# Seven products of quarters for eight in a decoder layer's output projection

## The chip, the cores and the metric

One core of one Trainium2 chip runs the kernel. The metric is the device time in microseconds, as the median of several executions. A core has a matrix engine (TensorE, PE in the profile), three engines for elementwise work (VectorE or DVE, ScalarE or ACT, GpSimd or POOL) and SyncE (SP), which issues most transfers. Each engine works through a queue of its own in order and waits on semaphores for the others. Matrix products accumulate in banks of PSUM, 128 rows of 512 floats each, which VectorE and ScalarE read.

## The reference

One decoder layer on 512 rows of width 1024, in float32. Cut to what matters here:

```python
u = rmsnorm(x, ln1_g)
q, k, v, pool_in, z, xbc, dt_raw, gate_pre = split(u @ w_in)
y_a = attention(q, k, v) @ w_a; y_b = pooling(pool_in) @ w_b; y_c = ssd(z, xbc, dt_raw) @ w_c
gates = sigmoid(gate_pre + b_gate)                       # three of width 1024
merged = gates[0] * y_a + gates[1] * y_b + gates[2] * y_c  # 512 x 1024
x = x + merged @ w_o                                     # the product changed here, w_o 1024 x 1024
x = x + conv_ffn(rmsnorm(x, ln2_g), ...)                 # up, depthwise conv, silu gate, down
out = rmsnorm(x, final_g)
```

## The kernel before, in words

The layer's rows are kept as four row blocks of 128, the columns as two halves of 512. A float32 product is made of three: each operand is split into a rounded high part and a remainder, and high x high, high x low and low x high are accumulated in one bank (`mm3`, L223 on; all its matmuls have line 236). Weights come through a pipeline of jobs (`Job`, the loop at the end of the function): while job n runs its matmuls, VectorE makes the remainder `wl` of job n+1 (`low`, L215), ScalarE casts the high part `wh` of job n+2 in two cuts (`cast`, L195), and SyncE fetches the raw weights of job n+3 (`fetch`, L182). There are two buffers for raw weights, three for `wh` and two for `wl`, so a step of this pipeline also waits for the buffer's former reader. Four engines (TensorE, ScalarE, VectorE, GpSimd) take their instructions in the order in which the program writes them out; SyncE's are placed by the framework. A list `running` holds generators, pieces of elementwise work that are carried on by one piece at each `step()`; the job bodies call `step()` after a bank or two. `after(n, it)` delays a piece by n steps.

Other products of the kernel already use 7 products of quarters where 8 would do (`Seven`, and `down_group` in the FFN). Rows of one operand and weights are then cut in quarters, and sums of quarters are multiplied; `sums_of` (L322 on) makes the four sums of an operand that are needed: four additions of half rows on VectorE, two casts on ScalarE, two remainders on VectorE.

The stage around the change:

- `branch_jobs(2, w_c, ...)`: four jobs of 48 matmuls, each two column blocks m of the branch's result. For each m, VectorE multiplies by the gate (L1226) and adds to the merged branches `MG[m]` (L1227), ScalarE casts the high part `mgh` (L1230), VectorE makes the remainder `mgl` (L1231).
- `load_x1`: SyncE loads both rows of norm gains and the eight pieces of x, `X1[tb, h]`.
- `wo_jobs(pair, h)`: the output product, for two row blocks (`pair`) and one half of the columns (`h`) at a time, in two jobs of four k each; 8 jobs of 24 matmuls. Each job fetches its 1 MB of w_o, so w_o is loaded twice. A finished bank is added to x by VectorE (L1252). After the first half, `norm_early` squares it on ScalarE and multiplies by the gain on GpSimd (L462). After the second half, `norm_late` squares that one (L437), takes the square root on ScalarE (L471, with a table load), forms the factor in four small VectorE operations (L486 to L490) and scales both halves into `us`. `norm_turn` then transposes them on TensorE (L451, 8 transposes a row block), and ScalarE and VectorE take high part and remainder out (L454, L455). For the first pair this comes a step later; for the second it is put into the opening of the FFN.
- `up_jobs`: the FFN. Its first two jobs (`opening`, L1421) begin with the columns of the first two row blocks while the norm of the last two is finished.

Of the kernel before, what the change touches and what calls it, by code (L numbers as in the profile page):

```python
# [10 lines left out]
F32 = mybir.dt.float32  # L11
F32R = mybir.dt.float32r
# [4 lines left out]
P = 128  # L17
S = 512
# [64 lines left out]
def trunk(ctx: ExitStack, tc, out, x, rel_bias, ln1_g, w_in, b_gate, w_a, pool_w, pool_scale, w_b,  # L83
# [370 lines left out]
            act.copy(hh, pv)  # L454
            dve.tensor_sub(ul[:, 4 * h:4 * h + 4, tb * P:(tb + 1) * P], pv, hh.bitcast(F32))  # L455

    def norm_early(t, g):

        ss, v0, xg = small("ss", [P, 1]), cpool.tile([P, 1], F32, name=f"v0_{len(V0)}"), T("xg")
        squares(act, t, ss)  # L460
        dve.tensor_scalar(v0, ss, 1.0 / D, EPS, OP.mult, OP.add)
        pool.tensor_tensor(xg, t, g[0], OP.mult)  # L462
        V0.append(v0)
        return v0, xg

    def norm_late(t, g, v0, outs, last=None):


        ss, v, sq, r, rt = (small(n, [P, 1]) for n in ("ss", "v", "sq", "r", "rt"))
        squares(act, t, ss)  # L470
        act.activation(sq, ss, AF.Sqrt, bias=v0, scale=1.0 / D)  # L471
        xg = T("xg")
        dve.tensor_tensor(xg, t, g[1], OP.mult)
        if last:
            dve.scalar_tensor_tensor(v, ss, -0.5 / D, last, OP.mult, OP.add)
            yield xg

            dve.reciprocal(r, sq)
            dve.scalar_tensor_tensor(rt, r, v, r, OP.mult, OP.mult)
            dve.scalar_tensor_tensor(rt, rt, 1.5, r, OP.add, OP.mult)  # L480

            (o1, x1), (o0, x0) = outs(xg)
            act.mul(o0, x0, rt)
            dve.tensor_scalar(o1, x1, rt, None, OP.mult)
            return
        dve.scalar_tensor_tensor(v, ss, 1.0 / D, v0, OP.mult, OP.add)  # L486
        yield xg
        dve.reciprocal(r, sq)
        dve.scalar_tensor_tensor(rt, r, v, r, OP.mult, OP.mult)
        dve.tensor_scalar(rt, rt, -0.5, 1.5, OP.mult, OP.add)  # L490
        for o, src in outs(xg):
            dve.tensor_scalar(o, src, r, rt, OP.mult, OP.mult)

    V0 = []

# [708 lines left out]
                    dve.tensor_sub(YT[q][1], Y[gi][:, q % 4, :], YT[q][0].bitcast(F32))  # L1204


    MG, MH, SG = {}, {}, {}

    def gate_jobs(b, lo=0, hi=8):
        def evac(m, ps):  # L1210
# [5 lines left out]

        return jobs_a(w_in, C_GATE + b * D + lo * P, hi - lo, uhk, ulk, KD, evac)

    def branch_jobs(b, w, parts, nk, last=False, more=()):
        def evac(m, ps):  # L1220
            if b == 1:
                MG[m] = T("yo")
                act.copy(MG[m], ps)
                return
            s = SG[b, m]
            dve.tensor_tensor(s, s, ps, OP.mult)  # L1226
            (dve if last else pool).tensor_tensor(MG[m], MG[m], s, OP.add)  # L1227
            if last:
                h, l = T("mgh", F32R), T("mgl", F32R)
                act.copy(h, MG[m])  # L1230
                dve.tensor_sub(l, MG[m], h.bitcast(F32))  # L1231
                MH[m] = (h, l)
# [8 lines left out]

    def load_x1():
        nxt["g2"] = grow(ln2_g[0])
        for tb in range(4):
            for h in range(2):
                t = X1[tb, h] = T("x1")
                sp.dma_start(t, x[tb * P:(tb + 1) * P, h * S:(h + 1) * S])

    def wo_jobs(pair, h):
        def evac(tb, ps):  # L1250
            t = X1[tb, h]
            dve.tensor_tensor(t, t, ps, OP.add)  # L1252
            if h == 0:
                nxt[tb] = norm_early(t, nxt["g2"])
                return
# [3 lines left out]
            v0, xg0 = nxt[tb]  # L1259
            us = [T("u0"), T("u1")]  # L1260
            it = norm_late(t, nxt["g2"], v0, lambda xg1: ((us[0], xg0), (us[1], xg1)))
# [20 lines left out]
        return jobs_b(lambda k0, k1: [wsrc(w_o, k0, k1, h * S, h * S + S)], S,  # L1282
                      lambda k, tb: MH[k][0][:, tb * P:(tb + 1) * P],
                      lambda k, tb: MH[k][1][:, tb * P:(tb + 1) * P], KD, evac,
                      blocks=(2 * pair, 2 * pair + 1), turn_over=pair == 1 and h == 1)


    ACTS = {}
    ff = {}
# [177 lines left out]
    def down_jobs(h):  # L1467

        def evac(tb, ps):
            t = X1[tb, h]  # L1470
            dve.tensor_tensor(t, t, ps, OP.add)
            if h == 0:
                running.append(early(tb))
                return
            v0, vh, xg0 = fin[tb]
            for _ in norm_late(t, fin["g"], v0, lambda xg1: ((xg1, xg1), (xg0, xg0)), last=vh):
# [14 lines left out]
    def program():  # L1491
# [21 lines left out]
        for group, next_ in zip(groups, groups[1:] + (None,)):  # L1513
# [4 lines left out]
            for i, job in enumerate(group.jobs):  # L1518
# [13 lines left out]
        yield from gate_jobs(0)  # L1532
        many = {"a": branch_jobs(0, w_a, AO, 3), "g": gate_jobs(2),
                "Z": z_jobs(0), "z": z_jobs(1)}
        for token in MIX:
            if token in many:
                yield next(many[token])
            else:
                yield Call(lambda i=int(token): waiting.append(y_norm(i)))
        yield Call(finish)  # L1540
        yield from branch_jobs(2, w_c, YT, 8, last=True)
        yield Call(load_x1)
        for pair in range(2):
            for h in range(2):
# [239 lines left out]
```

## Time and profile before

| what | value |
|---|---|
| median of 3 executions | 1021.73 us (1021.33 to 1021.78) |
| the profiled execution | 1021.86 us |
| its span in the trace | 1019.9 us |
| granted TensorE clock, mean | 0.998 |
| instructions | 13619 |

The page gives busy time by engine, the span in 40 slices, the chain of work that ended last, and the costliest groups of instructions by line. The timeline lists one engine's instructions in order: start, time, engine, line, operation, output and inputs, shapes, and in brackets the idle time ahead of it with what ended it. A name such as `pb` is the program's name of a tile: `pa` the banks of the w_c product, `pb` those of the output product, `pu` those of the FFN, `uT` transposes. Matmuls are pipelined, so a row's time is longer than the distance to the next row; the distances are used here.

### The profile page before, as it was taken

The numbers are of one execution on the slowest core, as the hardware profiler recorded it, in microseconds if no ns is written. First come the engines' busy times: TensorE is split into PE (matmuls) and PEld (weight loads), VectorE is DVE, ScalarE is ACT, GpSimd is POOL, SyncE is SP. The second block draws the span as 40 slices with busy tenths as digits, with TensorE's granted clock in tenths as the row PEclk, the third lists the DMA queues.
The fourth block names the chain that finished last, engine by engine and source line by source line (L and its number), as shares of the span: only waits on it lengthen the run. The fifth ranks groups of instructions, "written<-read, shape, count | busy, mean of one in ns | idle before, by whom it ended". The sixth has DMA issues, their size and how long they took to land.

```text
span 1019.9 us, 13619 instructions
## 1 busy us (share of the span) xinstructions
PE 1010.3 (99%) x5402; PEld 862.2 (85%) x5402; DVE 707.4 (69%) x886; ACT 511.3 (50%) x863; POOL 136.4 (13%) x120
## 2 busy tenths in 40 slices
PE   8999999999999999999999999999999999999997
PEld 8998878999988888888888888898888888888885
DVE  6564768577767647666889665768778768685756
ACT  5433546564435476879467224554444444433434
POOL 1691000010000000000052501102111100111002
PEclk9999999999999999999999999999999999999999
DMA  8548222255254344552253427532332322321332
GB/s 270 170 101 210 92 74 76 58 149 162 91 183 113 91 124 104 145 141 87 81 155 127 165 85 272 163 124 83 105 102 83 106 101 83 123 83 42 124 103 82
DMA packets 115629, 123.34 MB, mean 121 GB/s; under 512 B 6483, under 2 KB 96150, under 8 KB 115567
## 3 DMA queue, kind: packets, MB, share of 16 engines
q1 hardware_dynamic: 113247, 119.01, 37.5%
q0 software_dynamic: 1728, 2.62, 1.5%
q8 instruction: 42, 0.69, 0.3%
q10 hardware_dynamic: 592, 0.86, 0.2%
q14 instruction: 20, 0.16, 0.0%
HBM read 118.68 MB, written 3.00 MB: 119 GB/s over the span
## 4 chain that ended last, share of the span: by engine, by line
PE 98%; DMA 1%; DVE 0%; ACT 0%; ACTq 0%; issue 0%
PE pa L236 36%; PE pu L236 22%; PE pb L236 12%; PE pd L236 7%; PE pqk L236 6%; PE pq L236 3%; PE pa L1632 2%; PE ps L786 1%; PE pu L1421 1%; PE ppw L236 1%; PE po L834 1%; PE pt L820 1%; PE py L1119 1%; DMA xin<-in_x_dram 1%; PE pyo L1126 1%; PE pst L1107 0%
## 5 line engine op out<-in xcount | busy, mean ns | idle before, releaser
L215 DVE TENSOR_TENSOR wl<-raw,wh 128x2048 fp32r<-128x2048 f32 (+3 forms) x92 | 214.1, 2328 | 51.5 <-ACT wh L195 38.8
L195 ACT CAST wh<-raw 128x1024 fp32r<-128x1024 f32 (+4 forms) x181 | 181.4, 1021 | 57.4 <-DVE raw L359 17.8
L1316 DVE SCALAR_TENSOR_TENSOR hc<-pu,fcol,hc 128x510 f32<-128x510 f32 x88 | 65.9, 748 | 56.2 <-ACT hc L1313 54.5
L236 PE MATMUL pa<-uh,wh 128*128 128x512 f32 (+1 forms) x368 | 88.8, 381 | 0.0
L236 PE MATMUL pa<-ul,wh 128*128 128x512 f32 (+1 forms) x368 | 86.8, 375 | 0.0
L236 PE MATMUL pa<-uh,wl 128*128 128x512 f32 (+1 forms) x368 | 86.8, 375 | 0.0
L236 PE MATMUL pu<-uh,wh 128*128 128x512 f32 (+1 forms) x352 | 83.5, 379 | 0.0
L236 PE MATMUL pu<-ul,wh 128*128 128x512 f32 (+1 forms) x352 | 83.5, 379 | 0.0
L236 PE MATMUL pu<-uh,wl 128*128 128x512 f32 (+1 forms) x352 | 83.5, 379 | 0.0
L236 PEld LDWEIGHTS pa<-ul,wh 128*128 128x128 f32 x368 | 66.7, 188 | 12.6
L236 PEld LDWEIGHTS pa<-uh,wl 128*128 128x128 f32 x368 | 66.7, 188 | 12.5
L236 PEld LDWEIGHTS pa<-uh,wh 128*128 128x128 f32 x368 | 65.4, 189 | 11.8
L236 PEld LDWEIGHTS pu<-ul,wh 128*128 128x128 f32 x352 | 64.2, 188 | 12.5
L236 PEld LDWEIGHTS pu<-uh,wl 128*128 128x128 f32 x352 | 64.2, 188 | 12.5
L236 PEld LDWEIGHTS pu<-uh,wh 128*128 128x128 f32 x352 | 64.1, 188 | 12.4
L1313 ACT ACTIVATE hc<-pu,fcol,fcol 128x512 f32<-128x512 f32 x40 | 31.2, 779 | 78.9 <-PE pu L236 78.9
L1321 POOL TENSOR_TENSOR hc<-hc 128x512 f32<-128x512 f32 x22 | 30.8, 1400 | 289.1 <-DVE hc L1316 244.4
L808 ACT ACTIVATE sb<-sb,nmls 128x128 f32<-128x128 f32 (+1 forms) x72 | 30.0, 418 | 31.4 <-DVE nmls L805 20.8
L215 DVE TENSOR_TENSOR wl<-w,wh 128x2048 fp32r<-128x2048 f32 (+1 forms) x18 | 38.0, 2111 | 10.2 <-issue 4.6
L1102 POOL TENSOR_TENSOR st<-st,dts 128x512 f32<-128x512 f32 x4 | 4.2, 1052 | 225.6 <-ACT st L1110 163.5
L195 ACT CAST wh<-w 128x1024 fp32r<-128x1024 f32 (+1 forms) x36 | 32.9, 954 | 2.4 <-DVE w L341 2.4
L1318 ACT ACTIVATE hc<-hc 128x512 f32<-128x512 f32 x22 | 13.9, 633 | 40.2 <-DVE hc L1316 40.2
(409 smaller groups left out, 1924.4 us busy)
## 6 DMA issues: line engine op xcount, KB each, us to landing
raw<-in_w_in_dram SPq DMA_DIRECT2D x24, 1024.0 KB, 5.8
raw<-in_ffn_w_up_dram SPq DMA_DIRECT2D x22, 1024.0 KB, 5.7
raw<-in_w_o_dram SPq DMA_DIRECT2D x8, 1024.0 KB, 5.1
raw<-in_ffn_w_down_dram SPq DMA_DIRECT2D x8, 1024.0 KB, 5.3
raw<-in_w_in_dram SPq DMA_DIRECT2D x14, 512.0 KB, 5.5
raw<-in_w_in_dram SPq DMA_DIRECT2D x8, 768.0 KB
raw<-in_w_b_dram SPq DMA_DIRECT2D x4, 1024.0 KB
w<-in_ffn_w_down_dram SPq DMA_DIRECT2D x4, 1024.0 KB, 5.0
```

What stands on the lines that cost most here:

```text
L195: (other.tensor_copy if other and i else act.copy)(job.high[:, :, o], job.raw[:, :, o])
L215: (eng or dve).tensor_tensor(l[:, :, o], job.raw[:, :, o], h[:, :, o].bitcast(F32), OP.subtract)
L236: pe.matmul(ps, l, r, start=first and n == 0, stop=last and n == total - 1, skip_group_check=onto)
L786: pe.matmul(pss[i][:, o:o + w * P], q[r, n * P:(n + 1) * P], k[r, kb * P:(kb + w) * P], start=True, stop=True)
L808: act.activation(sb[:, off:off + w * P], sb[:, off:off + w * P], AF.Exp, bias=nm[:, n, h:h + 1], accum_out=ls[:, n, h:h + 1])
L820: pe.transpose(pt[:, o:o + P], sb[:, o:o + P], eye)
L834: pe.matmul(po[DH * hh:DH * hh + DH, n * P:(n + 1) * P], V[g, kb + i][:, (2 * c + hh) * DH:(2 * c + hh + 1) * DH], probs[2 * c + hh, nb][: ...
L1313: act.activation(t, ps, AF.Identity, bias=ff["c1"][:, ff["b"] + m:ff["b"] + m + 1], scale=fw(2, m))
L1316: dve.scalar_tensor_tensor(t[:, sh:], ps[:, :S - sh], fw(k, m), t[:, sh:], OP.mult, OP.add)
L1318: act.activation(t, t, AF.Silu)
L1321: pool.tensor_tensor(a, a, t, OP.mult)
L1632: pe.matmul(first[2 * n + j][:, lo:hi], a[:, k, j * P:(j + 1) * P], b[:, k, lo:hi], start=a is wh and b is uh and k == 0, stop=a is wl and ...
```

## The change

The 8 jobs of `wo_jobs` are replaced by the 7 of `wo_group`. Merged branches and w_o are cut in quarters: the rows of w_o in even and odd blocks of 128 (`two`), its columns in halves; the merged branches in the same blocks and in two halves of the rows. Every product is 2 row blocks x 4 k x 3 = 24 matmuls of 512 columns, on a pair of banks. They run in the order two, five, three, one, six, seven, four. `three` goes on in the banks of `five`; `six`, `seven` and `four` go on in those of `one`, and after each of them the banks are read while they still accumulate. Row blocks 0 and 1 are complete after `six`, 2 and 3 after `four`.

Of x, four pieces are loaded as before and added to by VectorE. The other four (`fresh`) are copied out of the bank by ScalarE, and x is added by an accumulating transfer that GpSimd issues. The norm's first half is now the one that is complete first, so `norm_early` and `norm_late` take its number; in the new form (`apart`) the late half is scaled by factor and gain in one VectorE operation, the early one by ScalarE.

Sums of weights: one by accumulating transfers (`plus`, four pieces of 256 KB), three by VectorE: `W[2]` in the w_c stage (`sums`), `W[1]` behind the remainder of `one`, and the sum of `four` when its cast is made, that is, while `six` is prepared. Sums of the merged branches are made in the w_c stage and at the start of the product (`merged`); `two` and `five` (`apart`) take their last k after the first three of both banks. One weight load for this product, `W[0]`, stands ahead in SyncE's queue where one of the FFN's stood, and so do three buffers of that pool, which the FFN's sums now get after it.

```diff
-    def norm_early(t, g):
+    def norm_early(t, g, h=0):
...
-    def norm_late(t, g, v0, outs, last=None):
+    def norm_late(t, g, v0, outs, last, h=1, apart=False):
...
+        xg = None
+        if not apart:
+            xg = T("xg")
+            dve.tensor_tensor(xg, t, g[h], OP.mult)
+        dve.scalar_tensor_tensor(v, ss, -0.5 / D, last, OP.mult, OP.add)
         yield xg
+
         dve.reciprocal(r, sq)
         dve.scalar_tensor_tensor(rt, r, v, r, OP.mult, OP.mult)
+        dve.scalar_tensor_tensor(rt, rt, 1.5, r, OP.add, OP.mult)
+
+        if apart:
+            o1, (o0, x0) = outs()
+            dve.scalar_tensor_tensor(o1, t, rt, g[h], OP.mult, OP.mult)
+            act.mul(o0, x0, rt)
+            return
...
+    def merged(m):
+        if m % 2 == 0:
+            t = T("m0", F32R)
+            act.copy(t[:, :256], MG[m][:, LO])
+            dve.tensor_sub(t[:, 256:], MG[m][:, LO], t[:, :256].bitcast(F32))
+            MH[m] = (t[:, :256], t[:, 256:])
+            return
+        h, l = T("mgh", F32R), T("mgl", F32R)
+        act.copy(h, MG[m])
+        it = sums_of(MG[m - 1], MG[m], T("sah", F32R), T("sal", F32R),
+                     lambda j, h, l: MS.__setitem__((j, m // 2), (h, l)), True)
+        if m < 7:
+            next(it)
+        dve.tensor_sub(l, MG[m], h.bitcast(F32))
+        MH[m] = (h, l)
+        if m > 6:
+            next(it)
+        yield
+        yield from it
...
+        for tb, h in ((0, 1), (1, 1), (2, 0), (3, 0)):
+            t = X1[tb, h] = T("x1")
+            sp.dma_start(t, x[tb * P:(tb + 1) * P, h * S:(h + 1) * S])
+
+    def wo_group():
...
+        def load():
+            for two in (0, 1):
+                W.append(ypool.tile([P, 4, S], F32, name="w3", tag="xs"))
+                sp.dma_start(W[-1], quarter(two, 1))
+            plus(0, 0, 0)
+
+        def plus(i, two, h):
+            for k in range(4):
+                pool.dma_start(W[i][:, k, :], quarter(two, h)[:, k, :], accum_op=OP.add)
+
+        def sums():
+            W.append(ypool.tile([P, 4, S], F32, name="w3", tag="xs"))
+            dve.tensor_tensor(W[2], W[0], W[1], OP.add)
+
+        def first(tb, h):
+            half = 1 - h
+            v0, xg = norm_early(X1[tb, half], nxt["g2"], half)
+            vh = cpool.tile([P, 1], F32, name=f"vo{tb}")
+            dve.tensor_scalar(vh, v0, -0.5, None, OP.mult)
+            nxt[tb] = v0, vh, xg
+
+        def then(tb, h):
...
-            if pair == 0:
+            if tb < 2:
                 r = rest()
                 next(r)
                 running.append(after(1, r))
...
+        def job(j, raw, form, bank, outs, more=False, op=OP.add, behind=None, apart=False, fresh=False):
...
+                def read(i):
+                    tb = 2 * hi + i
+                    if fresh:
+                        t = X1[tb, h] = T("x1")
+                        act.copy(t, bank[i])
+                        pool.dma_start(t, x[tb * P:(tb + 1) * P, h * S:(h + 1) * S],
+                                       accum_op=OP.add)
+                        return
+                    t = X1[tb, h]
+                    dve.tensor_tensor(t, t, bank[i], op)
+                    if behind:
+                        behind(tb, h)
+
+                if apart:
+                    for i in range(2):
+                        product(i, range(3), True, False)
+                    step()
+                    parts = side(j)
+                    for i in range(2):
+                        product(i, (3,), False, True)
+                        read(i)
+                    step()
+                    return
+                for i in range(2):
+                    product(i, range(4), True, True)
+                    read(i)
+                    step()
...
+        two = job("A12", quarter(1, 0), None, B, (0, 0), apart=True, fresh=True)
+        five = job(1, None, lambda: W[0], B, (1, 1), apart=True, fresh=True)
+        three = job(4, None, lambda: W[1], B, (0, 1), more=True)
+        one = job("A11", quarter(0, 0), None, A, (0, 0), behind=lambda tb, h: first(tb, 1))
+        six = job(2, None, lambda: W[2], A, (0, 1), more=True, op=OP.subtract, behind=then)
+        seven = job(3, None, lambda: W[1], A, (1, 1), more=True, op=OP.subtract,
+                    behind=lambda tb, h: first(tb, 0))
+        four = job("A22", quarter(1, 0), lambda: total(four.raw, four.raw, W[2]), A, (1, 0), more=True,
+                   behind=then)
+        one.then = lambda: total(W[1], W[2], one.raw, OP.subtract)
+        four.late, inner = True, four.body
...
-        yield from branch_jobs(2, w_c, YT, 8, last=True)
-        yield Call(load_x1)
-        for pair in range(2):
-            for h in range(2):
-                yield from wo_jobs(pair, h)
-            if pair == 0:
+        for i, job in enumerate(branch_jobs(2, w_c, YT, 8, last=True)):
+            if i == 1:
+                yield Call(sums)
+            if i == 3:
+                yield Call(load_x1)
+            yield job
+        for i, job in enumerate(group):
+            yield job
+            if i == 3:
                 yield Call(ff_cols)
...
-MIX = "ZZ0zz1ggggaa"
+MIX = "ZZ0zz1ggggwaa"
```

`four` is marked late: it is prepared as the old last job was (`late_split`), and its own preparation, the remainder of the FFN's first weights among it, is split over its end and the opening.

More of the change, by code (lines that the diff above doesn't have):

```diff
@@ L1228, in evac @@
             if last:
[L1229 to L1232, printed above, removed]
+                running.append(merged(m))
         return jobs_a(w, 0, 8, lambda k: parts[k][0], lambda k: parts[k][1], nk, evac,
@@ L1280, in evac, with body, product @@
                     pass
[L1282 to L1285, printed above, removed]
+        def job(j, raw, form, bank, outs, more=False, op=OP.add, behind=None, apart=False, fresh=False):
+            hi, h = outs
+            def body(ws):
+                wh, wl = ws
+                if not more:
+                    bank[:] = [MM("pb") for _ in range(2)]
+                parts = side(j)
+                def product(i, ks, begin, end):
+                    o = slice(i * P, (i + 1) * P)
+                    mm3(bank[i], lambda k: wh[:, k, :], lambda k: wl[:, k, :],
+                        lambda k: parts[k][0][:, o], lambda k: parts[k][1][:, o], ks, begin, end,
+                        flip=True, onto=more)
+                def read(i):
[14 more added lines that the diff above has]
+                    step()
+                    parts = side(j)
+                    for i in range(2):
[7 more added lines that the diff above has]
+                    step()
+            new = Job([raw] if raw is not None else [], 4, S, body)
+            new.form, new.once = form, True
+            if raw is None:
+                new.load = lambda: None
+            return new
@@ L1288, in trunk @@
+        return load, sums, [two, five, three, one, six, seven, four]
     ACTS = {}
@@ L1475, in evac @@
             v0, vh, xg0 = fin[tb]
-            for _ in norm_late(t, fin["g"], v0, lambda xg1: ((xg1, xg1), (xg0, xg0)), last=vh):
+            for _ in norm_late(t, fin["g"], v0, lambda xg1: ((xg1, xg1), (xg0, xg0)), vh):
                 xg1 = _
@@ L1534, in program @@
                 "Z": z_jobs(0), "z": z_jobs(1)}
+        load, sums, group = wo_group()
         for token in MIX:
-            if token in many:
+            if token == "w":
+                yield Call(load)
+            elif token in many:
                 yield next(many[token])
```

56 lines of the change are left out of this document (25 added, 31 removed).

## The prediction, made before the result

> **What bounds the kernel now.** I read the page's busy line first, then the chain of work that ended last, then the timelines of TensorE, VectorE and ScalarE from the product with w_c to the opening of the FFN.
>
> ```profile
> span 1019.9 us, 13619 instructions
> PE 1010.3 (99%) x5402; PEld 862.2 (85%) x5402; DVE 707.4 (69%) x886; ACT 511.3 (50%) x863; POOL 136.4 (13%) x120
> PEclk9999999999999999999999999999999999999999
> PE 98%; DMA 1%; DVE 0%; ACT 0%; ACTq 0%; issue 0%
> ...
> 616.02 27.20 PE pb L236 x120
> 643.23 1.75 PE uT L451 x16
> 644.97 10.91 PE pb L236 x48
> 656.19 5.64 PE pb L236 x24
> 661.83 3.83 PE pu L1421 x32
> 665.66 0.87 PE uT L451 x8
> 666.54 5.96 PE pu L1421 x48
> ```
>
> TensorE is busy 99% of the span and is 98% of the chain. The output product is the three pb rows: 120 + 48 + 24 = 192 matmuls, at 27.20 / 120 = 0.2267 us each. Between them stand only the 16 transposes (uT) of the next norm. So TensorE's queue sets the end, and every wait put into it is paid in full. The question is whether the shorter product still finds its operands ready.
>
> ```profile
> 615.86 1.07 PE L236 MATMUL pb<-wh,mgh 128*128 128x512 f32 x4
> 661.67 2.08 PE L1421 MATMUL pu<-uh,wh 128*128 128x256 f32 x16
> ```
>
> By TensorE's timeline the product starts at 615.86 and the opening of the FFN at 661.67: the stage takes 45.81 us. My sum is made on this clock.
>
> **The change part by part.** *TensorE.* Seven products of 24 matmuls stand for eight: 24 x 0.2267 = **5.44 us less**. Transposes and the two small turns of the FFN's columns stay, but move into the last products.
>
> *Up to the sixth product.* The products run in the order two, five, three, one, six, seven, four, each 5.44 us, in two halves of 12 matmuls (2.72 us), one for each of its two row blocks. VectorE gets the sums of the merged branches in the w_c stage. Their prices stand in the FFN, where the same helper runs:
>
> ```profile
> 738.09 0.41 DVE L326 TENSOR_TENSOR sa<-hc 128x256 f32<-128x256 f32 x1
> ...
> 739.21 0.42 DVE L329 TENSOR_TENSOR sb<-hc,sa 128x256 f32<-128x256 f32 x1
> L335 DVE TENSOR_TENSOR sal<-sa,sah x12: 679/681/693, 100.2 to 885.0; 128x512 fp32r<-128x512 f32 x12
> L341 DVE TENSOR_TENSOR raw<-raw,w x2: 2291/2292/2293, 850.7 to 963.8; 128x2048 f32<-128x2048 f32 x2
> 616.06 0.69 DVE L1226 TENSOR_TENSOR sg<-sg,pa 128x512 f32<-128x512 f32 x1 [2.58 <-PE pa L236]
> 616.85 0.69 DVE L1227 TENSOR_TENSOR yo<-yo,sg 128x512 f32<-128x512 f32 x1
> L1223 ACT COPY yo<-pa x8: 563/586/589, 128.1 to 181.0; 128x512 f32<-128x512 f32 x8
> ```
>
> A pair of merged rows costs 1.54 us of half-row sums (738.09 to 739.63), 2 x 0.68 us of remainders and 0.4 us for the quarter's remainder: 3.3 us. Less one 512-wide remainder (0.69) that goes, the w_c job of 10.88 us gets 2.6 us more, the second one also the weight sum of 2.29. VectorE idled 2.58 us ahead of each read of a bank (the L1226 row), two to a job, so I cost this at nothing but at the end of the stage. There, as built, VectorE has after the last addition (616.85 + 0.69 = 617.54): two remainders of the pair before (to 618.8), the last 512-wide one (619.5), the half-row sums (621.0), then the remainder of five's weights, 2.29 us, done at 623.2. TensorE needs it after two (621.30) and the 6 matmuls of five that do without: 622.66. **Wait 0.55.** Three accumulates onto five's banks; ScalarE must first have copied the first, 0.2 after its last matmul and 0.59 long, against the 0.68 us of the 3 matmuls that stand between: **0.17**. So six starts at T = 615.86 + 4 x 5.44 + 0.72 = 638.34 and not at 637.62.
>
> *Six, and the transposes behind it.* This is the step that decides. As built, TensorE's queue holds six's two halves, then at once the 8 transposes of row block 0, then seven's first half, the column turns, the transposes of block 1, seven's second half, four. The blocks' normalised rows u come from six's own result, so block 0's chain has only six's second half, 2.72 us, as cover. And the engines that make u are occupied. VectorE's queue holds, in order: read of one's block 1, its two norm scalars, remainder of seven's weights, the sum of four's weights, and only then the read of six's block 0. ScalarE's holds the two casts of that last sum, and only then the squares of six's block 0. The rows for each:
>
> ```profile
> 626.94 0.69 DVE L1252 TENSOR_TENSOR x<-x,pb 128x512 f32<-128x512 f32 x1 [1.09 <-PE pb L236]
> 628.42 0.15 DVE L461 TENSOR_SCALAR v<-ss 128x1 f32<-128x1 f32 x1 [0.79 <-ACT junk L437]
> 653.21 1.98 ACT L195 CAST wh<-raw 128x1024 fp32r<-128x1024 f32 x2
> 634.90 1.07 PE L236 MATMUL pb<-wh,mgh 128*128 128x512 f32 x4
> 635.10 0.69 DVE L1252 TENSOR_TENSOR x<-x,pb 128x512 f32<-128x512 f32 x1 [0.30 <-PE pb L236]
> 635.82 0.63 ACT L437 ACTIVATE junk<-x 128x512 f32<-128x512 f32 x1 [3.65 <-DVE x L1252]
> 636.57 1.28 ACT L471 ACT_TABLE_LOAD   x1
> 638.19 0.16 DVE L488 RECIPROCAL r<-sq 128x1 f32<-128x1 f32 x1 [1.45 <-ACT sq L471]
> 638.90 1.00 DVE L492 TENSOR_SCALAR u<-xg,r,rt 128x512 f32<-128x512 f32 x2
> L483 ACT ACTIVATE xg<-xg,rt x4: 722/724/725, 1004.8 to 1015.8; 128x512 f32<-128x512 f32 x4
> ```
>
> Counted from T: the read of one's block 1 starts 0.20 after its last matmul (634.90 to 635.10); the norm scalar 1.48 later (626.94 to 628.42), 1.68; the second, 1.9; seven's remainder starts at 2.1; four's sum starts at 4.4 and ends at 6.7 (2.29 each). ScalarE casts it until 8.7 (1.98). Without the casts the squares would start 0.72 after the read (6.7 + 0.72 = 7.4), so the casts cost 1.3. The squares start there, the reciprocal 2.37 later (635.82 to 638.19, the table load of 1.28 in it), 11.1; u another 0.71 (638.19 to 638.90), 11.8; ScalarE's half of u ends 0.72 and a hand-over later, at 12.6. TensorE was done with six at 5.44. **Wait 7.15 us.** In before, 5.44 us of another product stood there, and u lay in front of the transposes.
>
> *After it.* Transposes 0.87, seven's first half, turns 0.39, transposes, seven's second half: 20.2. Four's halves accumulate on the banks of seven, which VectorE must have read; but block 1 of six, its u, two remainders of block 0's transposes and four's 2.29 us remainder go first: the read ends at 20.45 (**wait 0.35**); the next, behind two column copies and two remainders more, at 23.95 where TensorE would go on at 23.24 (**0.78**). The FFN opens at T + 26.7 = 665.1, against 661.67: 3.4 later.
>
> ```profile
> 662.59 0.68 DVE L1252 TENSOR_TENSOR x<-x,pb 128x512 f32<-128x512 f32 x1
> 664.14 2.28 DVE L215 TENSOR_TENSOR wl<-raw,wh 128x2048 fp32r<-128x2048 f32 x1
> ```
>
> In before the opening's weight remainder ended at 666.42, just as TensorE wanted it (666.54). It stands behind the read of the last block, which now comes 1.6 after the opening's start and not 0.9: **0.7 more**.
>
> *At nothing.* Transfers: w_o is loaded in 6 MB and not 8; the adding ones are issued by GpSimd, some 0.9 us each:
>
> ```profile
> L356 POOL DMA_DIRECT2D w<-in_w_in_dram x12: 856/883/1573, 72.9 to 227.5; - x12
> DMA to landing us min/median/max: 3.6/6.2/9.0
> ```
>
> At most 9.0 us to landing; the x ones have 14 us from ScalarE's copy (621.5) to the read (635.8), those of the weights over 30. If one came 9 us late, it would hold VectorE there and cost about that. GpSimd's own products of x beside VectorE cost more:
>
> ```profile
> 537.63 4.91 POOL L884 TENSOR_TENSOR o<-o,wb 128x512 f32<-128x512 f32 x3 [0.20 <-DMA wb<-wd]
> 541.32 3.38 DVE L215 TENSOR_TENSOR wl<-raw,wh 128x2048 fp32r<-128x2048 f32 x1
> ```
>
> A remainder of 2.29 took 3.38 beside one. In the chain above such a product would overlap seven's remainder by 0.2 us, at most by all of it: 0 to 1.1 more. I take 0.1.
>
> *Sum.* -5.44 + 0.55 + 0.17 + 7.15 + 0.35 + 0.78 + 0.7 + 0.1 = **+4.4 us** on the profiled execution of 1021.86 (span 1019.9 and 1.96 around it), which lies 0.13 above the median, 1021.73. So **1026.1**.
>
> **The rivals.** *TensorE slows after the gap.* At its start, after idling, 128x128 matmuls ran at half the pace of the transposes above (5.29 / 24 = 0.22 against 1.75 / 16 = 0.11):
>
> ```profile
> 1.06 5.29 PE L1591 MATMUL pa<-ones 128*128 128x128 f32 x24 [1.06 <-DVE ones L1582]
> ```
>
> If 7.15 us of idling bring that back for 5.3 us, seven's first half ends 2.65 later. Most of it falls into waits that are there anyway (0.35 and 0.78, and the 0.7 of the opening); worked through, 0.8 stays: **1026.9**. Against it: the PEclk row grants 9 tenths or more in every slice, the first among them. The Trainium skill, "TensorE: Matmul & The Clock Gate", section "Part 1: The HAM clock gate", says that the clock halves after an idle window of some 3.4 us and needs as long a busy one to return. By that the gap here is long enough, and the loss is 1.7 us ahead of the waits, which would leave under 0.8; no run here yet shows such a gap in mid-kernel.
>
> *The chain is short (not slower).* Were the sum of four's weights, its casts and seven's remainder out of the way, six's read would start at 2.9, u be ready at 7.5, and the wait 2.1 instead of 7.15, with seven's and four's small waits gone: -5.44 + 0.72 + 2.1 + about 1 = -1.6, **1020.1**. It decides where u comes less than about 3 us after six's last matmul. Against it: the built order puts them ahead on two engines.
>
> *All waits hide.* Then the whole 5.44 is kept: **1016.3**. The transposes behind six speak against it.
>
> *More waits.* A late transfer of four's quarter, or GpSimd's products beside each of the four 2.29 us operations: 3 us more, **1029**.
>
> **How the numbers follow.** Forecast as summed 0.45; slowed clock 0.30; more waits 0.07; short chain 0.12; all hidden 0.06. Slower by over 0.2% (2.0 us, about what a measurement of this kernel can tell) holds the first three but for a tail of 0.03: 0.79. Within 0.2% gets that tail and 0.09 of the short chain, 0.12; faster the rest, 0.09. The range: low, the casts' 1.3 us and the small waits (1.9) do not show and a little more, 1022.0; high, the slowed clock and most of the further waits, 1029.0.
>
> **What would show it.** Right: 168 pb matmuls; an idle TensorE of about 7 us ahead of the first transposes of the next norm, ended by ScalarE's or VectorE's u; VectorE's 2048-wide sum directly ahead of six's first read; waits under 1 us at five and four. Wrong: transposes that start within 3 us of six's last matmul, or a larger gap earlier, in the w_c stage or at two, which I take to be covered.

## The result, and the profile after

The changed kernel takes **1025.68 us** (median of 6 executions, 1024.76 to 1026.36), the kernel before 1021.9 on the same chip (6 executions, 1021.33 to 1022.68): a ratio of 1.0036, 95% interval 1.0023 to 1.0049. The change makes the kernel 3.8 us slower. 1026.1 was forecast, with 1022.0 to 1029.0 as its range. The profiled execution took 1025.94 us.

The page of the changed kernel, its busy line, clock row and chain:

```profile
span 1024.2 us, 13621 instructions
PE 1007.2 (98%) x5378; PEld 858.4 (84%) x5378; DVE 718.8 (70%) x910; ACT 518.8 (51%) x877; POOL 141.3 (14%) x128
PEclk9999999999999999999999999899999999999999
PE 96%; DVE 2%; ACT 1%; DMA 1%; issue 0%; ACTq 0%; DVEq 0%
```

TensorE has the 24 matmuls less (5378 for 5402), yet the span is 4.3 us longer: VectorE and ScalarE now hold 3% of the chain, and slice 26 of the clock row reads 8. What TensorE waited for, over the whole span but for the kernel's first 10 us (engine, line, releaser: total, times, longest):

```profile
PE uT L451 <- ACT u L486: 6.9, 1, 6.9
PE pb L236 <- DVE wl L215: 0.3, 1, 0.3
```

TensorE's timeline from the last half of six to the opening of the FFN:

```profile
642.42 1.07 PE L236 MATMUL pb<-wl,sah 128*128 128x512 f32 x4
650.34 1.97 PE L451 MATMUL uT<-eye,u 128*128 128x128 f32 x8 [6.85 <-ACT u L486]
651.96 2.05 PE L236 MATMUL pb<-wh,sbh 128*128 128x512 f32 x4
653.81 1.91 PE L236 MATMUL pb<-wh,sbl 128*128 128x512 f32 x4
655.52 1.26 PE L236 MATMUL pb<-wl,sbh 128*128 128x512 f32 x4
656.62 0.27 PE L516 MATMUL fcol0p<-eye,fcol0r 128*128 128x128 f32 x1
...
666.14 2.08 PE L1531 MATMUL pu<-uh,wh 128*128 128x256 f32 x16
```

Two losses stand here. TensorE idles 6.85 us ahead of the transposes of row block 0. Then it works slowly: the 8 transposes take 1.62 us (650.34 to 651.96, against 0.87 a group in the kernel before) and seven's first half 4.66 (651.96 to 656.62, against 2.72). Why u comes late is seen on VectorE and ScalarE:

```profile
639.83 2.47 DVE L215 TENSOR_TENSOR wl<-w,wh 128x2048 fp32r<-128x2048 f32 x1
642.22 2.28 DVE L1376 TENSOR_TENSOR raw<-raw,w 128x2048 f32<-128x2048 f32 x1
644.42 0.68 DVE L1350 TENSOR_TENSOR x<-x,pb 128x512 f32<-128x512 f32 x1
...
648.86 0.16 DVE L479 RECIPROCAL r<-sq 128x1 f32<-128x1 f32 x1 [1.45 <-ACT sq L471]
```

```profile
644.61 1.99 ACT L195 CAST wh<-raw 128x1024 fp32r<-128x1024 f32 x2 [5.07 <-DVE raw L1376]
646.50 0.62 ACT L437 ACTIVATE junk<-x 128x512 f32<-128x512 f32 x1
647.24 1.28 ACT L471 ACT_TABLE_LOAD   x1
649.57 0.72 ACT L486 ACTIVATE u<-xg,rt 128x512 f32<-128x512 f32 x1 [0.74 <-DVE rt L481]
```

The first bank of six was complete when its second half began (640.61); VectorE reads it at 644.42, behind the remainder of seven's weights and the sum of four's (L1376). The squares (L437) could follow at 645.1 and start at 646.50, behind the two casts of that sum. This is the order that the prediction wrote down.

The slow pace shows when the clock row is asked in stretches of 4 us (PE busy and its instructions, PEclk, DMA share, GB/s):

```profile
640.00:644.00 4.00, 3.49 (x16) 1.00 0.07 15
644.00:648.00 4.00, 0.00 (x0) 0.70 1.01 360
648.00:652.00 4.00, 1.66 (x9) 0.50 0.39 149
652.00:656.00 4.00, 4.00 (x12) 0.52 0.00 0
656.00:660.00 4.00, 4.00 (x23) 1.00 0.33 93
```

If the clock is either whole or half, 0.70, 0.50 and 0.52 stand for 2.4, 4.0 and 3.8 us at half: 10.2 us, which begin inside the gap and outlast it by 5.5.

### The profile page after: what moved, and what is told of

Its sections match the earlier page's. It is cut to its first block, busy times and chain, and to the rows that moved or that the text cites. A ratio compares the mean times of both kernels' runs of the same rounds, so it can differ in the third digit from the quotient of the medians.

```text
span 1024.2 us, 13621 instructions
## 1 busy us (share of the span) xinstructions
PE 1007.2 (98%) x5378; PEld 858.4 (84%) x5378; DVE 718.8 (70%) x910; ACT 518.8 (51%) x877; POOL 141.3 (14%) x128
## 4 chain that ended last, share of the span: by engine, by line
PE 96%; DVE 2%; ACT 1%; DMA 1%; issue 0%; ACTq 0%; DVEq 0%
PE pa L236 35%; PE pu L236 22%; PE pb L236 11%; PE pd L236 7%; PE pqk L236 6%; PE pq L236 3%; PE pa L1748 2%; PE ps L784 1%; PE pu L1531 1%; PE ppw L236 1%; PE po L832 1%; PE pt L818 1%; PE py L1117 1%; DMA xin<-in_x_dram 1%; PE pyo L1124 1%; PE uT L451 0%
## 5 line engine op out<-in xcount | busy, mean ns | idle before, releaser
L215 DVE TENSOR_TENSOR wl<-raw,wh 128x2048 fp32r<-128x2048 f32 (+3 forms) x87 | 202.8, 2331 | 49.3 <-ACT wh L195 27.9
L195 ACT CAST wh<-raw 128x1024 fp32r<-128x1024 f32 (+4 forms) x171 | 171.6, 1021 | 71.4 <-DVE raw L359 17.8
L236 PEld LDWEIGHTS pa<-ul,wh 128*128 128x128 f32 x368 | 66.7, 188 | 12.6
L215 DVE TENSOR_TENSOR wl<-w,wh 128x2048 fp32r<-128x2048 f32 (+1 forms) x22 | 47.3, 2151 | 10.2 <-issue 4.6
L195 ACT CAST wh<-w 128x1024 fp32r<-128x1024 f32 (+1 forms) x44 | 41.0, 972 | 4.8 <-PE pb L236 2.4
```

The costliest lines, as they stand in the source:

```text
L195: (other.tensor_copy if other and i else act.copy)(job.high[:, :, o], job.raw[:, :, o])
L215: (eng or dve).tensor_tensor(l[:, :, o], job.raw[:, :, o], h[:, :, o].bitcast(F32), OP.subtract)
L236: pe.matmul(ps, l, r, start=first and n == 0, stop=last and n == total - 1, skip_group_check=onto)
```

## The experiments

**Theory.** The changed kernel loses its 5.44 us to a gap behind six, since the norm's chain of row block 0 has no product to cover it and lies behind a sum, a remainder and two casts in two queues. **Rival 1:** TensorE's half pace after the gap carries a good part of the loss. **Rival 2:** the loss comes from the added work and transfers as such, wherever they stand. All kernels below were compared with the kernel before on the same chip (1022.0 to 1022.1). The executions of the changed kernel spread over 1.6 us, so a difference to it of some tenths is read from the traces alone.

### The transposes two steps later

```diff
-                running.append(after(1, r))
+                running.append(after(3, r))
```

> The transposes of row blocks 0 and 1 are put two steps later: behind seven's second half and behind four's first half, instead of directly behind six. Theory A (the time is lost because TensorE's queue stands still behind six, and the VectorE work ahead of six's read is the reason): the single wait of 6.9 us goes, but seven and four accumulate on banks that VectorE reads late for the same reason, so about 1.8 us of wait come ahead of seven's first half, 3.0 ahead of its second and 1.9 ahead of four; no half pace, as each is shorter. About 3.4 us less than the changed kernel: 1022.3 us. Theory B (only the place of the transposes is wrong): all of the wait and the half pace go, 9.5 us less, 1016.3 us. Theory C (the added VectorE work and the adding transfers slow the stage wherever the transposes stand): 1025.7 us.

Measured: **1025.36**, ratio 1.0035 [1.0022, 1.0048]. The gap ahead of the transposes is gone, and the time is not back. TensorE's timeline:

```profile
646.28 1.17 PE L236 MATMUL pb<-wh,sbh 128*128 128x512 f32 x4 [1.75 <-DVE x L1350]
...
651.96 1.93 PE L236 MATMUL pb<-wh,sbh 128*128 128x512 f32 x4 [2.39 <-DVE x L1350]
653.69 1.91 PE L236 MATMUL pb<-wh,sbl 128*128 128x512 f32 x4
...
665.48 2.19 PE L1531 MATMUL pu<-uh,wh 128*128 128x256 f32 x16 [1.53 <-ACT uh L454]
```

The same queue holds TensorE at another door: seven goes on in the banks of six, and each must have been read by VectorE first. The first read still stands behind seven's remainder and four's sum, the second behind the norm chain of block 0. Then the later transposes let the opening wait. 1.75 + 2.39 + 1.53 = 5.7 us of waits for one of 6.85, and behind the second the 8 matmuls of 651.96 and 653.69 take 3.44 us where 1.81 is usual. So the place of the transposes alone is not the cause (theory B's 1016.3 falls); two of the three waits are for six's reads, and the third came with the move. Theory A's time, 1022.3, is missed by 3.1: it had neither the half pace nor the wait at the opening. By its time alone theory C (1025.7) would fit too; the next run decides between them.

### The sum of four's weights ahead of six

```diff
+        def opened(tb):
+            if tb == 0:
+                total(four.raw, four.raw, W[2])
+            first(tb, 1)
...
-        one = job("A11", quarter(0, 0), None, A, (0, 0), behind=lambda tb, h: first(tb, 1))
+        one = job("A11", quarter(0, 0), None, A, (0, 0), behind=lambda tb, h: opened(tb))
...
-        four = job("A22", quarter(1, 0), lambda: total(four.raw, four.raw, W[2]), A, (1, 0), more=True,
+        four = job("A22", quarter(1, 0), lambda: four.raw, A, (1, 0), more=True,
```

> The sum of four's weights is made behind the first read of one, while VectorE waits there, instead of ahead of six's read; nothing else moves, though the two casts of that sum on ScalarE no longer wait for it. Theory A: six's first read comes 2.2 us earlier, the squares 3.5 us earlier, so the wait ahead of the transposes is about 3.5 us instead of 6.9; if a gap of that length still halves the pace, half of that loss stays. 4 to 5 us less than the changed kernel: 1020.7 to 1021.7 us. Theory B (place of the transposes alone) and theory C (amount of work): the same work at another place, 1025.7 us.

Measured: **1022.46** (11 executions, 1021.39 to 1024.65), ratio 1.0006 [0.9997, 1.0015]: 3.2 us less than the changed kernel, by an order alone. The gap is down from 6.85 to 3.88. VectorE's reciprocal comes 8.00 us after the start of six (638.81 to 646.81), where it came after 10.97 (637.89 to 648.86). A slow stretch stands behind the gap:

```profile
648.29 1.17 PE L451 MATMUL uT<-eye,u 128*128 128x128 f32 x8 [3.88 <-ACT u L486]
649.14 2.03 PE L236 MATMUL pb<-wh,sbh 128*128 128x512 f32 x4
650.97 1.84 PE L236 MATMUL pb<-wh,sbl 128*128 128x512 f32 x4
652.64 1.09 PE L236 MATMUL pb<-wl,sbh 128*128 128x512 f32 x4
```

2.97 of the 6.85 us were the sum and its casts. No work was taken out, so rival 2 does not hold for them. The forecast, 1020.7 to 1021.7, is missed by 0.8: the gap is 0.4 longer than expected, and seven's first half still takes 4.43 us (649.14 to 653.57).

### The gap filled

The changed kernel, with 30 matmuls more behind six, whose results are not used, so that TensorE does not idle.

```diff
+                    if j == 2 and i == 1:
+                        spare = SM("spare")
+                        for n in range(30):
+                            pe.matmul(spare, parts[n % 4][0][:, :P], wh[:, n % 4, :],
+                                      start=True, stop=True)
```

> 30 matmuls of 512 columns into a bank that nobody reads are put between six and the transposes, so that TensorE works through the wait (30 x 0.2267 = 6.8 us); the result stays the reference's. Theory A with the half pace as a cost of its own: the transposes start when they did, then run at full pace, 2.7 us of matmuls and transposes are won, of which about 1.3 come back as waits for VectorE's reads of seven's banks and at the opening: 1.4 us less than the changed kernel, 1024.3 us. Rival (the slow pace behind the gap has another cause, such as VectorE's or ScalarE's traffic): 1025.7 us. Rival (nothing comes back): 1023.0 us.

Measured: **1025.18**, ratio 1.0029 [1.0018, 1.004]. The pace stays whole:

```profile
644.01 6.96 PE L1370 MATMUL spare<-wh,sah 128*128 128x512 f32 x30
651.03 1.09 PE L451 MATMUL uT<-eye,u 128*128 128x128 f32 x8
651.88 1.17 PE L236 MATMUL pb<-wh,sbh 128*128 128x512 f32 x4
...
655.35 1.25 PE L451 MATMUL uT<-eye,u 128*128 128x128 f32 x8 [0.17 <-DVE ul L455]
...
664.83 2.08 PE L1536 MATMUL pu<-uh,wh 128*128 128x256 f32 x16
...
669.99 2.18 PE L1536 MATMUL pu<-uh,wl 128*128 128x256 f32 x16 [0.29 <-DVE wl L215]
```

Six starts at 638.57 in this trace (T), the transposes come 12.46 us later as in the changed kernel (12.45), and the FFN opens at T + 26.26 instead of T + 28.25. So the half pace costs 2.0 us up to the opening. Of these 0.6 go again in the opening, which takes 13.80 us here and 13.24 there: without the delay, TensorE reaches VectorE's remainders (0.17 ahead of the opening, 0.29 in it) before they are done. So 1.4 us are left in the traces. The medians differ by 0.5, no more than their spread; by the time alone the forecast (1024.3) and the rival of another cause (1025.7) are both some 0.5 to 0.9 away. The pace decides: VectorE and ScalarE do the same work as in the changed kernel, and the pace is whole. Rival 1 is real, but small beside the gap.

### A gap of 2.3 us

The same with 20 matmuls in place of 30, so that a single gap of 2.3 us is left.

> The changed kernel with 20 in place of 30 idle-time matmuls behind six (their results are not used), so that TensorE stands some 2.3 us and not 0 ahead of the first transposes, with no other gap near. Theory R1 (a gap of some 2.4 us is enough to halve the pace for a while, as it seemed behind the gaps of 2.39 and 2.67 us in the kernels with later turns and reordered queues): seven's first half takes 3.5 us or more where it took 2.84 in the filled kernel. Theory R2 (it takes a longer gap, or two close together, as in those kernels): 2.9 us or less, time 1025.2 as in the filled kernel.

Measured: **1025.66** (4 executions), ratio 1.0036 [1.0021, 1.0051], as the changed kernel.

```profile
651.40 1.97 PE L451 MATMUL uT<-eye,u 128*128 128x128 f32 x8 [2.32 <-ACT u L486]
653.01 1.85 PE L236 MATMUL pb<-wh,sbh 128*128 128x512 f32 x4
```

```profile
648.00:652.00 4.00, 1.68 (x8) 0.88 0.75 253
652.00:656.00 4.00, 4.00 (x17) 0.69 0.00 0
```

2.32 us were enough, as theory R1 has it: the transposes take 1.61 us and seven's first half 3.54, against 0.85 and 2.84 in the filled kernel. By the clock (0.88 and 0.69) some 0.96 + 2.48 = 3.4 us ran at half.

### Turns at once in the kernel before

No part of the change but one: before's transposes are not put off by a product.

```diff
-                running.append(after(1, r))
+                running.append(r)
```

> The kernel before, with one thing taken over from the change: the transposes of row blocks 0 and 1 are not put off by one product, so they stand directly behind the product that makes their rows. Theory A (the loss of the change is the missing cover of the norm's chain, whatever the number of products): TensorE stands ahead of each of the two groups of transposes, some 2.3 and 2.6 us, and the time is 1026.8 though all eight products and no sum are there. If gaps of that length also halve TensorE's pace for a while, up to 1.7 us for each more: 1027 to 1030. Rival (the loss of the change comes from its extra sums and transfers): no change, 1022.0.

Measured: **1028.29** (4 executions), ratio 1.0055 [1.0039, 1.007], 6.3 us slower than the kernel before.

```profile
640.21 1.09 PE L451 MATMUL uT<-eye,u 128*128 128x128 f32 x8 [1.81 <-DVE u L492]
643.54 1.52 PE L451 MATMUL uT<-eye,u 128*128 128x128 f32 x8 [2.25 <-DVE u L492]
644.71 2.06 PE L236 MATMUL pb<-wh,mgh 128*128 128x512 f32 x4
646.57 1.52 PE L236 MATMUL pb<-wh,mgl 128*128 128x512 f32 x4
```

All eight products and no sum, and yet a loss of the same kind: 1.81 + 2.25 us of waiting, and 1.7 us of slow pace behind the second. The cover of the norm's chain is what counts, as the theory has it; rival 2 is not needed for this part.

### x by loads

```diff
-        for tb, h in ((0, 1), (1, 1), (2, 0), (3, 0)):
+        for tb, h in ((0, 0), (1, 0), (2, 1), (3, 1), (0, 1), (1, 1), (2, 0), (3, 0)):
...
-                        t = X1[tb, h] = T("x1")
-                        act.copy(t, bank[i])
-                        pool.dma_start(t, x[tb * P:(tb + 1) * P, h * S:(h + 1) * S],
-                                       accum_op=OP.add)
+                        t = X1[tb, h]
+                        dve.tensor_tensor(t, t, bank[i], op)
```

> The changed kernel with one part undone: the four tiles of x that it adds by transfers are loaded ahead and added by VectorE from the bank, as in the kernel before. The prediction costs these transfers at nothing, so this should give 1025.3 to 1026.3 (as the changed kernel); VectorE's four more reads (0.69 each) stand in the first products, where the reads of five's banks must come ahead of three and queue behind the remainder of five's weights: up to 1.5 more. Rival (the adding transfers delay the reads of x and with them the norm's chain): 1 to 3 us less than the changed kernel.

Measured: **1027.09** (4 executions), ratio 1.0046 [1.0033, 1.006], 1.4 us more than the changed kernel. A new wait stands at three, for VectorE's read of five's bank:

```profile
628.38 1.19 PE L236 MATMUL pb<-wh,sbh 128*128 128x512 f32 x4 [0.80 <-DVE x L1345]
...
651.92 1.97 PE L451 MATMUL uT<-eye,u 128*128 128x128 f32 x8 [6.92 <-ACT u L486]
653.54 1.82 PE L236 MATMUL pb<-wh,sbh 128*128 128x512 f32 x4
655.19 1.08 PE L236 MATMUL pb<-wh,sbl 128*128 128x512 f32 x4
```

The gap behind six is the same (6.92). So the adding transfers of x do not delay the norm's chain, and the rival (1 to 3 us less) falls. The wait of 0.80 is what VectorE's added reads cost, but it does not account for the 1.4 us. Behind the gap only the transposes (1.62) and the next four matmuls (1.65) are slow, a loss of 1.5 us where the changed kernel lost 2.7, and from the start of the product to the end of the opening this kernel takes 63.81 us (615.97 to 679.78), the changed one 64.15. Its profiled execution is longer ahead of this stretch (0.74 us) and behind it (0.60). Where the 1.4 us of the medians come from stays open.

### Reordered

The early sum, and the transposes of blocks 0 and 1 behind seven's second half and four's first half; the first scalar of the late norm is made with the others, so that VectorE goes from six's first read straight to its second.

```diff
-        dve.scalar_tensor_tensor(v, ss, -0.5 / D, last, OP.mult, OP.add)
-        yield xg
+        if apart:
+            yield xg
+            dve.scalar_tensor_tensor(v, ss, -0.5 / D, last, OP.mult, OP.add)
...
-                r = rest()
-                next(r)
-                running.append(after(1, r))
+                def spread():
+                    yield
+                    next(it, None)
+                    yield
+                    yield
+                    norm_turn(us, nxt["uh"], nxt["ul"], tb)
+
+                running.append(spread())
```

> Three moves together: the sum of four's weights behind the first read of one; six's second read directly behind its first, with the norm's factor of both blocks after them; the transposes of blocks 0 and 1 behind seven's second half and four's first. Theory A: the waits ahead of the transposes, seven and four shrink to about 0.2, 0.5 and 0.5 us and one of 1 us at the opening; no half pace. The opening comes about 8.5 us earlier than in the changed kernel: 1017.2 us, 4.7 below the kernel before. Theory C: 1025.7 us. If it comes out between, the trace shows which bank's read is late.

Measured: **1021.72** (11 executions, 1019.95 to 1024.61), ratio 0.9999 [0.9989, 1.0009]: 4 us less than the changed kernel, but 4.5 more than expected. The gaps behind six are gone (0.15 is left), one stands ahead of the opening, and the pace is slow behind it:

```profile
661.04 3.61 PE L1545 MATMUL pu<-uh,wh 128*128 128x256 f32 x16 [2.67 <-ACT uh L454]
664.45 2.18 PE L1545 MATMUL pu<-ul,wh 128*128 128x256 f32 x16
```

ScalarE's queue has the casts of the transposes behind the squares of four's blocks, which wait for VectorE's reads. What I had not worked through was the queue behind the place from which I took the work. Whether each execution pays the slow pace there is open, as one was traced. The mean granted clocks on record fit with some that do not: 0.995 in the three executions of 1024.03 us and more, 0.996 in the traced one (1022.41), 0.997 to 0.999 in the seven below 1022, and 0.998 or 0.999 in all 23 of the kernel before on that chip.

### Three moves

On top of that, for that one wait: the remainder of four's weights goes behind seven's first bank read, and in four the step with the transposes and their casts comes ahead of the first bank read.

```diff
                     product(i, range(4), True, True)
+                    if j == "A22" and i == 0:
+                        step()
+                        read(i)
+                        continue
                     read(i)
                     step()
+                    if j == 3 and i == 0:
+                        seven.prepare()
...
+        seven.late = True
```

> Two more moves on top of the reordered kernel, in which TensorE still stood 2.7 us ahead of the FFN's opening (for ScalarE's uh, 660.42 to 661.47, queued behind the squares of the fourth product's row blocks) and then ran the first 16 matmuls of the opening in 3.41 us instead of 1.92. The remainder of four's weights goes behind seven's first bank read, and in four the transposes of block 1 are emitted ahead of the bank read. Theory A (what is left are waits of the order of the queues alone): the wait of 2.8 and the slow pace of 1.5 both go, the opening begins some 41.8 us after the product (44.6 in the reordered kernel, 45.8 in the kernel before), time 1017.4 against 1022.0 of the kernel before. Theory B (the engines' work in this stage is simply too much for the shorter product, and a wait that goes comes back in the next place): some 1020 to 1022, with a new wait of 2 us or more in the opening.

Measured: **1019.04** (5 executions, 1018.98 to 1020.02), ratio 0.9967 [0.9954, 0.9979]: 3.0 us faster than the kernel before and 6.6 than the changed one. Its page counts as many instructions of TensorE, VectorE, ScalarE and GpSimd as that of the changed kernel (5378, 910, 877 and 128). So rival 2 falls: the same work in another order beats both. TensorE's waits from the product on, but for the one at five:

```profile
PE pu L1552 <- DVE wl L215: 0.8, 1, 0.8
PE pb L236 <- DVE wl L215: 0.6, 2, 0.4
PE pb L236 <- DVE x L1359: 0.2, 1, 0.2
```

From product to opening it takes 42.39 us (615.82 to 658.21), before 45.81, after 50.91. The 0.36 and 0.79 that came back at four and in the opening, 1.5 us by the distances of the rows, are most of the 1.6 us missing to theory A's 1017.4.

### Two moves more

```diff
                 late.append(rest())
-                for _ in late_split.pop(0):
-                    pass
...
+                    if j == "A22":
+                        if i == 0:
+                            step()
+                            read(i)
+                            continue
+                        for _ in late_split.pop(0):
+                            pass
                     read(i)
-                    step()
                     if j == 3 and i == 0:
                         seven.prepare()
+                    step()
```

> Two more moves in VectorE's queue, for the two waits that the kernel with three moves still shows: the remainder of four's weights directly behind seven's first bank read (TensorE waited 0.36 us for it, ending 653.50), and the remainder of the opening's weights ahead of the last bank read (TensorE waited 0.79 us, ending 663.81). Theory A (they are waits of order alone): both go, 1019.0 - 0.36 - 0.7 = 1017.9 to 1018.1. Theory B (a wait that goes comes back behind it): 1018.7 to 1019.2, with a new wait for the last block's transposes, whose read then comes 2.3 us later.

Measured: **1019.31** (8 executions), ratio 0.9971 [0.9961, 0.9982]: no difference to the three moves. Four's wait is gone, and the opening's has grown and got a second:

```profile
664.19 2.18 PE L1553 MATMUL pu<-uh,wl 128*128 128x256 f32 x16 [1.00 <-DVE wl L215]
...
671.33 2.18 PE L1553 MATMUL pu<-uh,wl 128*128 128x256 f32 x16 [0.25 <-DVE wl L215]
```

Here theory B holds, in its time nearly (1018.7 to 1019.2) and in that a wait comes back, though not ahead of the last block's transposes, where it was looked for: what is left moves with the order and does not go. How VectorE's queue would have to look to lose it was not tried.

## Why the prediction was right

On the stage's own clock, with T the start of six (637.89 after, 638.57 with the gap filled):

| step | predicted | changed kernel | gap filled |
|---|---|---|---|
| matmuls of the product | 24 fewer, -5.44 | 24 fewer | |
| wait at five | 0.55 | 0.25 | 0.25 |
| start of product to T | 22.48 | 22.66 | 22.68 |
| wait ahead of block 0's transposes | 7.15 | 6.85 | (filled) |
| T to those transposes | 12.6 | 12.45 | 12.46 |
| seven's first half | 2.72 | 4.66 | 2.84 |
| waits at four | 0.35 + 0.78 | none | under 0.1 |
| T to the opening | 26.7 | 28.25 | 26.26 |
| the opening | 14.1 (0.7 more) | 13.24 | 13.80 |

**The deciding step held.** Wait, cause and queue order behind six are those of the text: VectorE's 2048-wide sum directly ahead of six's first read, ScalarE's casts ahead of the squares, u the last to come. The experiments bear it out from three sides: the sum moved away takes 2.97 us off the gap, the kernel before loses 6.3 us when its cover is taken away, and an order that gives cover turns the loss into a gain.

**The first rival came true beside the forecast, which had left it out.** I gave the slowed clock 0.30 and argued against it from the clock row, which "grants 9 tenths or more in every slice". A slice is 25.5 us long, and the kernel before has no gap in mid-kernel: the row could not speak on it. Nor does it show the slow start by which the rival was priced: in stretches of 1 us it reads 1.00 there, while the 24 matmuls take their 5.29 us; why is open. The loss was priced at 2.65 and came to 2.7 (1.94 in seven's first half and 0.75 in the transposes), partly by luck: with x by loads the same gap cost 1.5. It makes the opening 2.0 us later than in the filled kernel, where 0.8 was to stay; of it 1.4 are left after the opening, and 0.5, no more than the spread, in the medians. The Trainium skill, "TensorE: Matmul & The Clock Gate", section "Part 1: The HAM clock gate", has a window of some 3.4 us that does not start with the kernel, and a halved clock after an idle one. The traces agree with the window's length: 10.2 us at half are three of it, the 6.8 with x by loads (648.1 to 654.9) two, and the 3.4 us behind the short gap one. That a whole window must be idle they do not bear out (2.32 us were enough).

**The small terms were too large.** 0.55 at five, 0.35 and 0.78 at four and 0.7 in the opening are 2.4 together. The changed kernel shows only 0.25, since the slow pace made TensorE late for the others; in the filled kernel they are 0.25, under 0.1 and 0.29 (0.41, 0.08 and 0.53 by the distances of the rows). In the filled kernel VectorE's two reads end at T + 20.1 and 23.35 (20.45 and 23.95 forecast), and TensorE comes to four at T + 20.6 (20.2 forecast): a few tenths each way, in terms that were themselves differences of a few tenths. GpSimd's product beside seven's remainder, put at 0.1, made it 2.47 us for 2.29.

**So the number is better than its parts, and in part by luck.** From the start of the product to the end of the opening the sum says 63.3 us (22.48 + 26.7 + 14.1). The filled kernel, which has no slow pace, takes 62.74 (615.89 to 678.63), so the terms are 0.6 too large together. The changed kernel takes 64.15 (615.23 to 679.38), as the slow pace that was left out adds 1.4; the kernel before takes 59.25 (615.86 to 675.11). Two errors of opposite sign leave 0.85. On its own clock, moreover, the sum is 4.2 (3.4 + 0.7 + 0.1) and not 4.4: 0.15 us of before's 45.81 are neither matmuls nor transposes nor turns, and no term takes them off.

And the stage began 0.63 us earlier than in the trace of before. It comes from the kernel's first 10 us, which the change does not touch: a load of x took 5.68 us there and not 6.38, and the second group of transposes starts at 9.54 and not 10.24. In the ten traces taken after the prediction the stage begins between 615.23 and 616.56, as much as a third of the loss apart, and in each of them 605.6 to 605.8 us after that group.

**At nothing.** That the transfers would cost nothing held: no idle time of TensorE, VectorE or ScalarE in this stage is ended by one, and with x loaded ahead the gap is no shorter.

## What to carry to other kernels

Before a product is made shorter, ask what it covered: here 5.44 us of matmuls hid the norm's chain, and without a new place for that chain the saving came back as a gap. Where a wait goes, write out the queues of all engines behind it once more, accumulating banks among them; two orders that looked good on one queue lost their gain on the next. And a gap of TensorE can cost more than its length: behind each gap of 2.3 us or more that was traced here, some 1.5 us of work or more went to the slow pace, unless waits behind it took that up.

## What the runs showed of the hardware

- In the traces, gaps of TensorE of 2.32, 2.67, 3.88, 6.85 and 6.92 us were followed by half pace, and so were two close together (1.75 and 2.39, 1.81 and 2.25), behind the second. Behind the first of those pairs (1.75, 1.81) the pace stayed whole. The filled kernel, without a gap, stayed at 1.00.
- Behind the gaps of up to 3.88 us the half pace lasts some 3.4 us and costs 1.5 to 1.7 us of work. Behind the two long ones it differs: 5.5 us were left of it after 6.85 us of idling, which cost 2.7, and 3.0 us after 6.92, which cost 1.5. So the length of the gap alone does not set the loss.
- The slow stretch need not begin with the first matmul behind the gap: after 3.88 us of idling the 8 transposes took 0.85 us, the usual time, and the matmuls behind them 1.83 in place of 0.91.
